# Attention in a hybrid encoder block: the softmax rows of a tile's two halves lie end to end, one transpose turns the last half block of the first with the first half block of the second, and the turned blocks lie in fixed tiles

## The chip, the cores and the metric

The kernel runs on one core of one Trainium2 chip (trn2). The metric is device time in microseconds: a program is run several times and the median is taken. Below, PE is the TensorE matmul queue, PEld its weight loads, DVE is VectorE, ACT ScalarE, POOL GpSimd, and SP the engine that issues most DMAs.

## What is computed

One encoder block over 1024 positions and 16 meta tokens, width 1024: an RMS norm, one input projection, a retention branch, an attention branch, gates, an output projection and a second norm. The change touches the attention branch alone, so that part of the reference is shown:

```python
def _windowed_sink_attention(q, k, v, sink):
    ...
    ok = (jnp.abs(qpos[:, :, None] - kp) <= WINDOW) & (kp >= CHUNK) & (kp < Lp)
    s_band = jnp.einsum("bnqgrd,bnkgd->bngrqk", qb, kb) * scale
    s_band = jnp.where(ok[None, :, None, None], s_band, NEG_INF)
    s_meta = jnp.einsum("bnqgrd,bmgd->bngrqm", qb, km) * scale
    s = jnp.concatenate([s_band, s_meta], axis=-1)
    ...
    p = jnp.exp(s - m)
    p = p / (jnp.sum(p, axis=-1, keepdims=True) + jnp.exp(sink_l - m))
    o = (jnp.einsum("bngrqk,bnkgd->bnqgrd", p[..., :3 * CHUNK], vb)
         + jnp.einsum("bngrqm,bmgd->bnqgrd", p[..., 3 * CHUNK:], vm))
```

There are 8 query heads of 128 channels, 2 key heads, 8 blocks of 128 positions, and a window of 128 positions on either side. All is float32. The kernel keeps that precision by splitting an operand into a rounded high part and the rest (names that end in h and l), so that a product takes three matmuls: high by high, low by high, high by low (`mm3`).

## The kernel before

The program runs in stages on one core: projections and retention first (up to about 335 us), then attention (about 335 to 546 us), then the gate projections, the two branch projections and the output projection. In the last stages PE multiplies 512 columns at a time.

**The attention.** A tile is a pair of heads `hp` (four of them) and a block `n` (eight), so 32 tiles. A tile has two sides `x_` of 128 rows, each of 64 queries of both heads. Side 0 sees the whole of block n-1, the whole of block n and the first 64 keys of block n+1; side 1, 64 positions on, sees the last 64 keys of block n-1, the whole of n and the whole of n+1. With 16 meta keys this makes 336 scores in a row (272 or 208 at the two ends).

`stage1(hp, n)` makes the scores of both sides on PE (`ps`), masks them on DVE and takes the row's extreme (`raw`, `nm`), takes exp on ACT with the row's sum (`p`, `den`), inverts the sum on DVE, scales the row on POOL, and copies the 16 meta columns twice into `pm2` on POOL. The last two tiles scale on ACT instead.

`stage2(hp, n)` turns the weights, so that keys lie on partitions. Each side's row lies in a field of 401 columns with 64 zeros at one end, so that each of the three blocks is 128 columns wide for both sides: 2 transposes for each block, 4 into the PSUM bank `t1` and 2 into `t2` (those of n+1), and one of the meta columns. For n = 0 and n = 7 there are two blocks, so 4 and one. ACT copies `t1` into `pah` (high part, 512 columns), the meta rows into `pm` and the third block into `pbh` (256 columns). DVE makes the low parts `pal`, `pm` and `pbl`.

`stage3(hp, n)` multiplies by the values: three matmuls of 256 columns for each block and one for the meta keys, summed in `po`, which ACT copies out.

**What sets the order.** The loop over the 32 tiles issues, for tile k: `stage1` of tile k+1, `stage2` of tile k, a counted number of pieces of other work (`fill`: the projections `paq` and `pak` of later heads and the products `pe` of the gates), and `stage3` of tile k-1. PE keeps that order through `follow`. So a tile's weights are turned one whole tile after its scores, and are used one tile later still. Other engines' instructions are put in order by the framework, which plans with a model of each instruction's length; a change of lengths can move instructions past one another there. POOL's queue holds the scaling of `p` and also the accumulating DMAs that rotate the queries and keys (`aq<-m_aq`, `akr<-m_ak`).

The lines that the prediction names are 1486 (mask), 1489 (exp), 1496 (inverse), 1505 (scaling), 1525, 1529 and 1530 (transposes), 1535, 1538 and 1545 (ACT's copies), 92 (DVE's low parts, a helper), 76 to 78 (`mm3`), 1560 and 1565.

## Time and profile before

| what | before |
|---|---|
| time, median of 3 runs | 1032.83 us (1031.2 to 1034.33) |
| span of the profiled execution, first to last instruction | 1029.8 us |
| DMA, moved in the span | 188.45 MB, mean 183 GB/s |
| attention (335 to 546 us): instructions on the turned tiles (`pt`) | PE 28.83, DVE 50.39, ACT 40.18 us busy |
| attention: instructions on the softmax rows (`p`) | PE 25.34, ACT 38.95, POOL 42.66 us busy |

The profile gives the span of the execution that it took and no time for what lies around it; the median of the runs is 3.0 us above that span. A busy time of PE is the sum of matmuls whose ends are modelled and which overlap: two neighbours can start 0.11 us apart and be listed with 0.27 us each, so what a matmul occupies is read from the distance of two starts in the timeline, and not from its length. A row of the timeline gives start, length, engine, source line, operation and tiles; "x4" merges four instructions that followed each other without a gap, and square brackets hold the idle time ahead of it and what ended it.

### The profile page before, as it was taken

What the parts mean: (1) busy time and instruction counts of PE and PEld (TensorE: products, weight loads), DVE (VectorE), ACT (ScalarE), POOL (GpSimd) and SP (SyncE); (2) the same over time, 40 slices, a digit from 0 to 9 for tenths busy, and PEclk for the clock granted to TensorE, in tenths of its full rate; (3) what the DMA queues carried; (4) which work ended last, traced back from release to release, by engine and by line L of the source; (5) the groups of instructions that cost most, each with busy time, mean ns of one, the idle gap of its engine ahead of it and who ended that gap; (6) DMA issues with size and microseconds to landing.
All of it is one profiled execution on the core that took longest, in us unless ns stands there. A gap on an engine that the chain in (4) does not pass through costs nothing. (4 is left out here: it accounts for less than half of the span.)

```text
span 1029.8 us, 17327 instructions
## 1 busy us (share of the span) xinstructions
PE 1019.0 (99%) x5875; PEld 898.0 (87%) x5875; DVE 834.5 (81%) x1805; ACT 505.0 (49%) x1138; POOL 228.3 (22%) x368
## 2 busy tenths in 40 slices
PE   9999999999999999999999999999999999999997
PEld 8999999989989888988888888888887888888886
DVE  7787858769866778777769999998889899778665
ACT  5632332523424566665677555455567456334442
POOL 3445244243342424443310000000000000111032
PEclk9999999999999999999999999999999999999999
DMA  9433123243241457675559689899874856889464
GB/s 354 172 88 88 62 46 89 82 88 101 80 94 62 103 164 203 177 196 163 172 175 329 204 286 326 303 320 317 273 259 145 261 197 200 246 213 354 123 122 81
DMA packets 98984, 188.45 MB, mean 183 GB/s; under 512 B 13040, under 2 KB 37648, under 8 KB 98336
## 3 DMA queue, kind: packets, MB, share of 16 engines
q1 hardware_dynamic: 81344, 162.89, 46.9%
q0 software_dynamic: 10176, 14.73, 9.5%
q10 hardware_dynamic: 7376, 9.73, 2.8%
q8 instruction: 46, 0.75, 0.3%
q14 instruction: 42, 0.34, 0.1%
HBM read 124.32 MB, written 57.68 MB: 177 GB/s over the span
## 5 line engine op out<-in xcount | busy, mean ns | idle before, releaser
L1348 POOL DMA_DIRECT2D mx_d<-c1a x4 | 3.6, 890 | 391.2 <-DMA a<-in_w_out_dram 369.3
L77 PE MATMUL bz<-big,llz 128*128 128x512 f32 x192 | 74.9, 390 | 0.2 <-DVE llz L92 0.2
L78 PE MATMUL bz<-big,lhz 128*128 128x512 f32 x192 | 74.4, 389 | 0.0
L76 PE MATMUL bz<-big,lhz 128*128 128x512 f32 x192 | 74.1, 389 | 0.0
L76 PE MATMUL pv<-wh,big 128*128 128x256 f32 x256 | 73.0, 285 | 0.0
L78 PE MATMUL pv<-wl,big 128*128 128x256 f32 x256 | 72.7, 284 | 0.0
L77 PE MATMUL pv<-wh,big 128*128 128x256 f32 x256 | 72.3, 282 | 0.0
L77 PE MATMUL bz<-T,llz 128*128 128x512 f32 x176 | 68.6, 390 | 0.6 <-DVE llz L92 0.6
L78 PE MATMUL bz<-T,lhz 128*128 128x512 f32 x176 | 68.5, 389 | 0.0
L76 PE MATMUL bz<-T,lhz 128*128 128x512 f32 x176 | 68.3, 390 | 0.0
L1505 POOL TENSOR_SCALAR p<-p,den 128x336 f32<-128x336 f32 (+2 forms) x60 | 33.0, 572 | 83.5 <-DVE den L1496 78.7
L76 PE MATMUL paq<-big,wh 128*128 128x512 f32 x128 | 51.5, 402 | 0.0
L1489 ACT ACTIVATE p<-raw,nm 128x337 f32<-128x337 f32 (+1 forms) x64 | 35.5, 556 | 32.1 <-DVE nm L1486 30.7
L77 PE MATMUL paq<-big,wl 128*128 128x512 f32 x128 | 50.3, 393 | 0.0
L78 PE MATMUL paq<-big,wh 128*128 128x512 f32 x128 | 50.3, 393 | 0.0
L76 PEld LDWEIGHTS pv<-wh,big 128*128 128x128 f32 x256 | 48.4, 189 | 0.2
L77 PEld LDWEIGHTS pv<-wh,big 128*128 128x128 f32 x256 | 48.4, 189 | 0.0
L78 PEld LDWEIGHTS pv<-wl,big 128*128 128x128 f32 x256 | 48.3, 189 | 0.0
L77 PEld LDWEIGHTS bz<-big,llz 128*128 128x128 f32 x192 | 36.0, 188 | 7.9 <-DVE llz L92 0.5
L78 PEld LDWEIGHTS bz<-big,lhz 128*128 128x128 f32 x192 | 36.1, 188 | 7.4
L76 PEld LDWEIGHTS bz<-big,lhz 128*128 128x128 f32 x192 | 36.1, 188 | 7.4
L558 ACT ACTIVATE op<-pa,rcol 128x256 f32<-128x256 f32 x32 | 15.2, 475 | 53.6 <-PE pa L78 52.7
(627 smaller groups left out, 3612.4 us busy)
## 6 DMA issues: line engine op xcount, KB each, us to landing
wrz<-in_w_in_dram SPq DMA_DIRECT2D x32, 512.0 KB, 5.7
wr<-in_w_in_dram SPq DMA_DIRECT2D x29, 512.0 KB, 3.7
we<-in_w_in_dram SPq DMA_DIRECT2D x16, 512.0 KB, 4.5
tg<-tg_d SPq DMA_DIRECT2D x32, 256.0 KB, 5.2
e<-e ACTq DMA_DIRECT2D x20, 256.0 KB, 2.8
e<-e SPq DMA_DIRECT2D x20, 256.0 KB, 4.4
xn<-in_x_dram SPq DMA_DIRECT2D x8, 512.0 KB, 9.4
oTr_d<-ost SPq DMA_DIRECT2D x16, 256.0 KB, 2.1
```

The lines of the kernel that those rows point to most:

```text
L76: nc.tensor.matmul(o, ah, bh, start=first, stop=False, **kw)
L77: nc.tensor.matmul(o, al, bh, start=False, stop=False, **kw)
L78: latest[:] = [nc.tensor.matmul(o, ah, bl, start=False, stop=last, **kw).ins]
L558: nc.scalar.activation(o, pa[:, 0:256], AF.Copy, scale=rcol[:, c:c + 1])
L1348: nc.gpsimd.dma_start(d, to, accum_op=ALU.add)
L1489: last["exp"] = nc.scalar.activation(pp[:, x_, w0 - o:w0 - o + 1 + wid], r[:, 0:1 + wid], AF.Exp, scale=-1.0, bias=nm_[:, x_:x_ + 1], accu ...
L1505: nc.gpsimd.tensor_scalar(v, v, den[:, x_:x_ + 1], 1.0, op0=ALU.mult, op1=ALU.mult)
```

## The change

The two sides' rows now lie end to end in one row of 674 columns (`weights`), side 0 in columns 1 to 336 and side 1 from column 337 on. The last 64 columns of side 0 (block n+1) and the first 64 of side 1 (block n-1) are neighbours, and one transpose turns both: on partitions 0 to 63 it has side 0's half of block n+1, on 64 to 127 side 1's half of block n-1. That makes 4 whole blocks, this shared one and the meta columns, so 6 transposes in place of 7 for n = 1 to 6. For n = 0 and n = 7 there are 5 as before; for n = 0 the shared one has 64 columns. The halves that nobody writes hold zeros, set once.

The turned blocks go into fixed tiles `pth` and `ptl` of 6 x 128 columns, one pair for even and one for odd n, in place of `pah`, `pal`, `pbh` and `pbl` from a pool of two. ACT copies the 4 whole blocks at once (3 for n = 0 and 7) and each half block, 64 partitions by 128 columns, on its own; DVE does the same for the low parts. In stage 3 a block's two sides are now two runs of 128 columns, which touch for block n and are 512 columns apart for n-1 and n+1. The number and the shape of stage 3's matmuls stay.

```diff
@@ -1441,15 +1441,21 @@
     late_mask = aw.tile([P, 320], F32, name="late_mask")[:, 0:272]
     nc.vector.memset(late_mask, 0.0)
     nc.vector.tensor_copy(late_mask[:, 192:256], mask[0][:, 272:336])
-    weights = [ap.tile([P, 2, 401], F32, name=f"p{i}") for i in range(2)]
-    for t in weights:
-        nc.vector.memset(t[:, 0, 337:401], 0.0)
-        nc.vector.memset(t[:, 1, 0:64], 0.0)
+    weights = [ap.tile([P, 674], F32, name=f"p{i}") for i in range(2)]
+    ap.tile([P, 48], F32, name="space_t")
+    turned = [[ap.tile([P, 6 * P], R, name=f"pt{s}{i}") for s in "hl"] for i in range(2)]
+    for i in range(2):
+        for t in turned[i]:
+            nc.vector.memset(t[64:128, 0:P].bitcast(F32), 0.0)
+            nc.vector.memset(t[0:64, 5 * P:6 * P].bitcast(F32), 0.0)
 
     def attention():
         oa = [None]
         raw = [aw.tile([P, 337], F32, tag=f"raw{x_}", bufs=1, name=f"raw{x_}") for x_ in range(2)]
         st1, st2 = {}, {}
+
+        def blocks_own(n):
+            return 0 if n == 0 else P if n % 2 else P + NM
 
         def window(n, x_):
 
@@ -1482,11 +1488,11 @@
                 r = raw[x_]
                 for c in ({0: (272, 336), 7: (208,)} if x_ else {0: (0,)}).get(n, ()):
                     nc.vector.tensor_copy(r[:, c:c + 1], nsink[:, hp:hp + 1])
-                o, w0 = (0, 64) if x_ else (1, 1)
+                o, w0 = (0, 337) if x_ else (1, 1)
                 scored = nc.vector.tensor_tensor_reduce(r[:, o:o + wid], s[:, 0:wid], seen, -SCALE,
                                                         nsink[:, hp:hp + 1], ALU.add, ALU.min, nm_[:, x_:x_ + 1]).ins
 
-                last["exp"] = nc.scalar.activation(pp[:, x_, w0 - o:w0 - o + 1 + wid], r[:, 0:1 + wid], AF.Exp,
+                last["exp"] = nc.scalar.activation(pp[:, w0 - o:w0 - o + 1 + wid], r[:, 0:1 + wid], AF.Exp,
                                                    scale=-1.0, bias=nm_[:, x_:x_ + 1],
                                                    accum_out=den[:, x_:x_ + 1]).ins
                 sides.append((wid, w0, blocks, moff))
@@ -1498,13 +1504,13 @@
             both = ap.tile([P, 2, 2, NM], F32, tag="pm2", bufs=2, name=f"pm2_{hp}_{n}")
             ends = hp == 3 and n > 5
             for x_, (wid, w0, _, _) in enumerate(sides):
-                v = pp[:, x_, w0:w0 + wid]
+                v = pp[:, w0:w0 + wid]
                 if ends:
                     softmax.append(nc.scalar.activation(v, v, AF.Copy, scale=den[:, x_:x_ + 1]).ins)
                 else:
                     nc.gpsimd.tensor_scalar(v, v, den[:, x_:x_ + 1], 1.0, op0=ALU.mult, op1=ALU.mult)
             for x_, (_, w0, _, moff) in enumerate(sides):
-                w_ = pp[:, x_, w0 + moff:w0 + moff + NM].unsqueeze(1).to_broadcast([P, 2, NM])
+                w_ = pp[:, w0 + moff:w0 + moff + NM].unsqueeze(1).to_broadcast([P, 2, NM])
                 if ends:
                     softmax.append(nc.scalar.copy(both[:, x_], w_).ins)
                 else:
@@ -1513,42 +1519,46 @@
                 with tc.issue_after(last["scaled"]):
                     while held:
                         held.pop(0)()
-            pt = [lambda o, x_=x_, w0=w0: pp[:, x_, w0 + o:w0 + o + P] for x_, (_, w0, _, _) in enumerate(sides)]
-            st1[hp, n] = (pt, [b for _, _, b, _ in sides], both.rearrange("p a b c -> p (a b c)"))
+            own, late = blocks_own(n), 337 - (64 if n else 0)
+            cuts = [1] * (n > 0) + [1 + own, late + own] + [late + 272] * (n < NB - 1 and n > 0) + [late + P] * (n == 0)
+            ends_ = (1 + P, 1 + P + 64) if n == 0 else (273, 273 + P)
+            st1[hp, n] = ([pp[:, c:c + P] for c in cuts], pp[:, ends_[0]:ends_[1]], both.rearrange("p a b c -> p (a b c)"))
 
         def stage2(hp, n):
-            pt, sides, both = st1.pop((hp, n))
-            blocks = sides[0]
+            full, ends_, both = st1.pop((hp, n))
             t1 = p1(f"pt1_{hp}_{n}")
-            for j in range(2):
-                for x_ in range(2):
-                    nc.tensor.transpose(t1[:, 256 * j + P * x_:256 * j + P * x_ + P], pt[x_](sides[x_][j][1]), ident)
+            c0 = 0 if n else P
+            for j, v in enumerate(full):
+                nc.tensor.transpose(t1[:, c0 + P * j:c0 + P * j + P], v, ident)
+            c1 = c0 + P * len(full)
             t2 = p1(f"pt2_{hp}_{n}")
-            if len(blocks) > 2:
-                for x_ in range(2):
-                    nc.tensor.transpose(t2[:, 256 + P * x_:256 + P * x_ + P], pt[x_](sides[x_][2][1]), ident)
+            nc.tensor.transpose(t2[0:64 if n == 0 else P, P:2 * P], ends_, ident)
             latest[:] = [nc.tensor.transpose(t2[0:4 * NM, 0:P], both, ident).ins]
-            ah = ap.tile([P, 512], R, tag="pah", bufs=2, name=f"pah{hp}_{n}")
-            al = ap.tile([P, 512], R, tag="pal", bufs=2, name=f"pal{hp}_{n}")
+            th, tl = turned[n % 2]
 
             m = pm[n % 2]
-            nc.scalar.copy(ah, t1)
+            nc.scalar.copy(th[:, P + c0:P + c1], t1[:, c0:c1])
             heads = [(slice(32 * e_, 32 * e_ + 32), slice(P * e_, P * e_ + P)) for e_ in range(2)]
             for r, c in heads:
                 last["hi"] = nc.scalar.copy(m[r, c], t2[r, 0:P]).ins
-            bl = []
-            for j in range(2):
-                bl.append((blocks[j][0], ah[:, 256 * j:256 * j + 256], al[:, 256 * j:256 * j + 256]))
-            if len(blocks) > 2:
-                bh_ = ap.tile([P, 256], R, tag="pbh", bufs=2, name=f"pbh{hp}_{n}")
-                bl_ = ap.tile([P, 256], R, tag="pbl", bufs=2, name=f"pbl{hp}_{n}")
-                last["hi"] = nc.scalar.copy(bh_, t2[:, 256:512]).ins
-                bl.append((blocks[2][0], bh_, bl_))
-            dve_lo(al, t1, ah)
+            edges = []
+            if n < NB - 1:
+                edges.append((slice(0, 64), slice(0, P)))
+            if n:
+                edges.append((slice(64, 128), slice(5 * P, 6 * P)))
+            for r, c in edges:
+                last["hi"] = nc.scalar.copy(th[r, c], t2[r, P:2 * P]).ins
+            dve_lo(tl[:, P + c0:P + c1], t1[:, c0:c1], th[:, P + c0:P + c1])
             for r, c in heads:
                 last["lo"] = dve_lo(m[64 + r.start:64 + r.stop, c], t2[r, 0:P], m[r, c])
-            if len(blocks) > 2:
-                last["lo"] = dve_lo(bl_, t2[:, 256:512], bh_)
+            for r, c in edges:
+                last["lo"] = dve_lo(tl[r, c], t2[r, P:2 * P], th[r, c])
+            bl = []
+            for b, c in ((n - 1, P), (n, 2 * P), (n + 1, 0)):
+                if 0 <= b < NB:
+                    step = P if b == n else 4 * P
+                    bl.append((b, *(t.rearrange("p (x q) -> p x q", q=P)[:, c // P:c // P + step // P + 1:step // P]
+                                    for t in (th, tl))))
             st2[hp, n] = (bl, m)
 
         def stage3(hp, n):
@@ -1556,7 +1566,8 @@
             bl, m = st2.pop((hp, n))
             po = p3(f"po{hp}_{n}")
             for j, (b, h_, l_) in enumerate(bl):
-                mm3(po[:, 0:256], *(t[:, P * g:P * g + P] for t in (vah[:, b], low_value(b))), h_, l_, j == 0, False)
+                mm3(po[:, 0:256].rearrange("p (x q) -> p x q", x=2),
+                    *(t[:, P * g:P * g + P] for t in (vah[:, b], low_value(b))), h_, l_, j == 0, False)
             latest[:] = [nc.tensor.matmul(po[:, 0:256], vm[:, P * g:P * g + P], m, start=False,
                                           stop=True).ins]
             if n % 2 == 0:
```

Where instructions stand in the built programs, at three places. First PE, the scores of tile (2, 4) and the transposes of tile (2, 3); `ps_4_1` are scores, `pt_2_3` the turned weights, `p` the softmax rows, `pm_2_3` the meta columns. Before:

```order
L77 MATMUL ps_4_1_6646<-kTh_6211,aql_1_6357 128x336
L78 MATMUL ps_4_1_6646<-kTl_6212,aqh_1_6356 128x336
L1525 MATMUL pt_2_3_6658<-ident,p_4895 128x128
L1529 MATMUL pt_2_3_6663<-ident,p_4895 128x128
L1525 MATMUL pt_2_3_6658<-ident,p_4895 128x128 x3
L1529 MATMUL pt_2_3_6663<-ident,p_4895 128x128
L1530 MATMUL pt_2_3_6663<-ident,pm_2_3_6570 64x128
```

And now:

```order
L77 MATMUL ps_4_1_6613<-kTh_6187,aql_1_6330 128x336
L78 MATMUL ps_4_1_6613<-kTl_6188,aqh_1_6329 128x336
L1532 MATMUL pt_2_3_6625<-ident,p_4895 128x128 x4
L1535 MATMUL pt_2_3_6630<-ident,p_4895 128x128
L1536 MATMUL pt_2_3_6630<-ident,pm_2_3_6540 64x128
```

Six transposes of 128 columns have become five; what stands ahead of and behind them is the same work. Over the whole program PE has 24 matmuls fewer.

Second DVE, the low parts of the same tile; `den` is the inverse of the row sums, `m_aq` and `aq` the rotation of a later head's queries, `we` a weight. Before:

```order
L1496 RECIPROCAL den_4_6639<-den_4_6639 128x2
L92 TENSOR_TENSOR pal_3_6668<-pt_2_3_6658,pah_3_6667 128x512
L92 TENSOR_TENSOR pm_4888<-pt_2_3_6663,pm_4888 32x128 x2
L92 TENSOR_TENSOR pbl_3_6673<-pt_2_3_6663,pbh_3_6672 128x256
L838 TENSOR_TENSOR we_1_6520<-we_0_6519,we_1_6520 128x4x128
L188 TENSOR_TENSOR m_aq_00_6691<-paq_00_6609,sr 128x512
L189 TENSOR_TENSOR aq_00_6690<-paq_00_6609,cr 128x512
```

And now:

```order
L1502 RECIPROCAL den_4_6606<-den_4_6606 128x2
L92 TENSOR_TENSOR ptl_4900<-pt_2_3_6625,pth_4899 128x512
L188 TENSOR_TENSOR m_aq_00_6655<-paq_00_6576,sr 128x512
L189 TENSOR_TENSOR aq_00_6654<-paq_00_6576,cr 128x512
L92 TENSOR_TENSOR pm_4888<-pt_2_3_6630,pm_4888 32x128 x2
L92 TENSOR_TENSOR ptl_4900<-pt_2_3_6630,pth_4899 64x128 x2
L838 TENSOR_TENSOR we_1_6490<-we_0_6489,we_1_6490 128x4x128
```

One instruction of 256 columns on 128 partitions has become two of 128 columns on 64 partitions, and at this tile the rotation stands ahead of them. ACT's copies change in the same way (`pbh`, 128x256, becomes two `pth`, 64x128), at every tile with n = 1 to 6.

Third POOL, around the scaling of tile (1, 6); `akr<-m_ak` are DMAs that POOL issues for the rotated keys. Before:

```order
L89 TENSOR_SCALAR pm_1_5_6026<-p_4895 128x32 x2
L193 DMA akr_0_6058<-m_ak_0_6059 64x272 x2
L1505 TENSOR_SCALAR p_4894<-p_4894,den_6_6109 128x336 x2
L193 DMA akr_1_6158<-m_ak_1_6159 64x256 x2
L89 TENSOR_SCALAR pm_1_6_6123<-p_4894 128x32 x2
```

And now:

```order
L89 TENSOR_SCALAR pm_1_5_6008<-p_4895 128x32
L193 DMA akr_0_6037<-m_ak_0_6038 64x272
L193 DMA akr_1_6134<-m_ak_1_6135 64x256 x2
L1511 TENSOR_SCALAR p_4894<-p_4894,den_6_6088 128x336 x2
L89 TENSOR_SCALAR pm_1_6_6102<-p_4894 128x32 x2
```

The scaling of tile (1, 6) now stands behind the two DMAs of `akr_1`, which it stood ahead of. From the end of attention on, some instructions of ACT, DVE and SP have changed places with neighbours, and on PE a few matmuls; their number and kinds are the same.

## The prediction

> **What bounds the kernel now.** I begin with the page: the shares of the engines and the granted clock.
>
> ```profile
> span 1029.8 us, 17327 instructions
> PE 1019.0 (99%) x5875; PEld 898.0 (87%) x5875; DVE 834.5 (81%) x1805; ACT 505.0 (49%) x1138; POOL 228.3 (22%) x368
> PEclk9999999999999999999999999999999999999999
> ```
>
> PE is busy for 1019.0 of 1029.8 us, and its clock is at its top in each slice but for rounding. A busy PE need not be an unbroken one, so the view by stages comes next: attention, then the two halves of what follows up to the last matmuls.
>
> ```profile
> 335.00:546.00 211.00, 210.33 (x1277) 187.17 (x1276) 162.56 (x417) 130.93 (x351) 71.23 (x151) 1.00 0.61 172
> 546.00:785.00 239.00, 239.00 (x1055) 197.82 (x1054) 220.09 (x363) 134.47 (x239) 0.00 (x0) 1.00 0.81 280
> 785.00:1023.00 238.00, 237.27 (x1057) 196.52 (x1055) 194.39 (x332) 108.86 (x203) 26.20 (x31) 1.00 0.69 201
> ```
>
> The columns are the stage, its length, then busy time of PE, PEld, DVE, ACT and POOL, the clock, and the DMA share and rate. In attention PE is busy 210.33 of 211.00 us, while DVE has 48 us free (211.00 - 162.56) and ACT 80. Behind attention PE is as full, with DVE at 92% in the first half (220.09 of 239). So the question is what a PE instruction less is worth, whether the other engines keep up, and whether the stages behind pass the gain on. The view of the chain that ended last reaches only the closing DVE work, so it decides nothing here.
>
> **What a transpose occupies.** The groups give its listed length, the timeline the distance of two starts (tile (0, 5)).
>
> ```profile
> L1525 PE MATMUL pt<-ident,p 128*128 128x128 f32 x128 | 19.8, 274 | 0.3 <-POOL p L1505 0.2
> L1529 PE MATMUL pt<-ident,p 128*128 128x128 f32 x48 | 9.7, 274 | 0.1
> ```
>
> ```profile
> 369.54 0.60 PE L1525 MATMUL pt<-ident,p 128*128 128x128 f32 x4
> 369.98 0.38 PE L1529 MATMUL pt<-ident,p 128*128 128x128 f32 x2
> 370.19 0.27 PE L1530 MATMUL pt<-ident,pm 128*64 128x128 f32 x1
> 370.22 0.48 PE L76 MATMUL pe<-big,weh 128*128 128x512 f32 x1
> 370.54 0.39 PE L77 MATMUL pe<-big,wel 128*128 128x512 f32 x1
> 370.77 0.40 PE L78 MATMUL pe<-big,weh 128*128 128x512 f32 x1
> ```
>
> Four start within 0.44 us (369.98 - 369.54) and two within 0.21, so six in 0.65: 0.108 us each. The listed 274 ns overlap. The transpose of the meta columns loads 64 columns where the others load 128; it and the matmul of 512 columns behind it take 0.35 (370.54 - 370.19), of which that matmul by itself has 0.23 (370.77 - 370.54). The 0.12 left are no less than a full one's 0.108, so a transpose of 64 columns is not cheaper.
>
> **The removed transposes.** One goes at each tile with n = 1 to 6, in four head pairs: 24. At n = 0 and 7 the count stays at five, and the narrow one at n = 0 saves nothing by the row above. 24 x 0.108 = **2.6 us** off PE, in a stage where PE hardly waits: the group's idle time ahead of 128 transposes is 0.3 us.
>
> The Trainium skill, page "TensorE: Matmul & The Clock Gate", section "Part 4: PE-mode transpose", gives about 275 ns for a transpose in a kernel's context and says that the full clock does not engage for it. The first agrees with the listed 274 ns here, and the second finds no support in the clock row; priced so, 24 would be 6.6 us, and the sum 1026.2.
>
> **What ACT and DVE get.** Where one copy of 128x256 was, two of 64x128 stand. The trace has none of 64x128; the nearest row has 128 columns on 32 partitions. From the timeline at tile (1, 3), with POOL's rows for later:
>
> ```profile
> 414.83 0.52 ACT L1538 CAST pm<-pt 32x128 fp32r<-32x128 f32 x2
> 415.36 0.37 ACT L1545 CAST pbh<-pt 128x256 fp32r<-128x256 f32 x1
> 415.60 0.67 DVE L92 TENSOR_TENSOR pal<-pt,pah 128x512 fp32r<-128x512 f32 x1
> 415.63 0.63 ACT L698 CAST aqh<-aq 128x512 fp32r<-128x512 f32 x1
> 416.14 1.69 POOL L193 DMA_DIRECT2D aq<-m_aq  x2 [7.67 <-ACT pbh L1545]
> 416.30 0.58 DVE L92 TENSOR_TENSOR pm<-pt,pm 32x128 fp32r<-32x128 f32 x2
> 416.90 0.42 DVE L92 TENSOR_TENSOR pbl<-pt,pbh 128x256 fp32r<-128x256 f32 x1
> 417.24 0.68 DVE L92 TENSOR_TENSOR aql<-aq,aqh 128x512 fp32r<-128x512 f32 x1
> 417.26 1.66 POOL L1505 TENSOR_SCALAR p<-p,den 128x336 f32<-128x336 f32 x2
> ```
>
> On ACT two of 128 columns take 0.53 us (415.36 - 414.83) and one of 256 takes 0.27 (415.63 - 415.36); on DVE 0.60 (416.90 - 416.30) and 0.34 (417.24 - 416.90). Each engine gets 0.26 us a tile, 24 x 0.26 = 6.2 us in all. At n = 0 and 7 a half block's copy is added and the large one loses 128 of 512 columns; that is at most another 0.3 us for each of 8 tiles, 2.4. Together 8.6 us on engines with 48 and 80 free. The bounds for a tile are 0 (a copy of 64 partitions as short as half of the large one) and 0.53 on DVE, if its low parts also wait for ACT's later copies of the same bank. Even 0.53 x 24 = 12.7 us leaves DVE room, so as throughput this costs **nothing**: PE's products of other heads cover it, and without that cover it would cost the 6.2 us. Four more memsets, ahead of attention, have DVE's own waits there to lie in.
>
> **Where it can be felt** is on tiles where PE gets to the transposes just as POOL has scaled. Three show it in PE's timeline: (1, 4), (2, 2) and (2, 3).
>
> ```profile
> 418.63 0.27 PE L1529 MATMUL pt<-ident,p 128*128 128x128 f32 x1
> 418.98 0.55 PE L1525 MATMUL pt<-ident,p 128*128 128x128 f32 x3
> ```
>
> ```profile
> 454.19 0.60 PE L1525 MATMUL pt<-ident,p 128*128 128x128 f32 x4
> 454.86 0.41 PE L1529 MATMUL pt<-ident,p 128*128 128x128 f32 x2
> ```
>
> ```profile
> 461.24 0.27 PE L1529 MATMUL pt<-ident,p 128*128 128x128 f32 x1
> 461.74 0.55 PE L1525 MATMUL pt<-ident,p 128*128 128x128 f32 x3 [0.23 <-POOL p L1505]
> ```
>
> Against 0.11 a transpose the steps are long by 0.24 (0.35 - 0.11), 0.23 (0.67 - 0.44) and 0.39 (0.50 - 0.11), 0.86 in all. The chain behind them is mask on DVE, exp on ACT, inverse on DVE, scaling on POOL, so 0.26 us more ahead of it can lengthen each stall by 0.26: 0 to 0.8 us for three. The new order also needs side 1's scaling at the third transpose, not the second, which gives 0.1 back. At tile (1, 6) POOL's scaling now stands behind two DMA issues:
>
> ```profile
> 426.87 1.07 POOL L1505 TENSOR_SCALAR p<-p,den 128x336 f32<-128x336 f32 x2 [2.98 <-DVE den L1496]
> 427.89 1.64 POOL L193 DMA_DIRECT2D akr<-m_ak  x2
> 430.61 0.60 PE L1525 MATMUL pt<-ident,p 128*128 128x128 f32 x4
> ```
>
> Swapped, the DMAs go from about 427.0, when DVE has the key, to 428.7; the scaling runs from 1.1 us after their start, as in the rows of 416.14 and 417.26, to 429.8, or 430.3 with the meta copies behind it. PE is there at 430.5. That still fits, with a price of 0 to 0.6. I take **0.4 us** for all four places, half of the 0.8, the 0.6 being covered.
>
> **Behind attention.** The gain survives if the next stage starts earlier too.
>
> ```profile
> 540.00 0.69 DVE L1057 TENSOR_TENSOR stz0S<-wrz,wrz 128x512 f32<-128x512 f32 x1 [3.37 <-PE pe L78]
> 541.52 0.40 PE L76 MATMUL bz<-big,lhz 128*128 128x512 f32 x1
> 542.08 0.50 PE L77 MATMUL bz<-big,llz 128*128 128x512 f32 x1 [0.16 <-DVE llz L92]
> 785.47 0.39 PE L76 MATMUL br<-big,lhr 128*128 128x512 f32 x1
> 786.44 0.50 PE L77 MATMUL bz<-T,llz 128*128 128x512 f32 x1 [0.58 <-DVE llz L92]
> ```
>
> DVE sat idle 3.37 us and began the next stage's operands when PE had done its last `pe` product, so that start moves with PE. PE then waits for `llz` at 542.08 (0.33 over its step of 0.23) and once more at 786.44 (0.74 over), and nowhere between, so DVE keeps ahead for 244 us. Stages behind pass the gain on, as far as those two waits are not set by a DMA.
>
> **Sum.** On the span: 1029.8 - 2.6 + 0.4 = 1027.6. The median of the runs is 3.0 above the span, so **1030.6 us**, 0.2% less than 1032.83. About 0.3%, or 3.1 us, is what a measurement of this kernel can tell from no change, and the three runs lie 3.1 apart.
>
> **Rivals.**
>
> *The gain turns into waits* (0.13). PE comes 0.11 us a tile earlier to rows that ACT and DVE finish 0.26 later, and 2.6 us earlier to `llz`. For it speaks DVE's 92% from 546 to 785, against it that PE waits only twice there. If it takes all: 1032.8.
>
> *Stalls go as well* (0.12). The framework has laid ACT, DVE and SP anew; without the 0.86 of the three tiles, the 0.33 and the 0.74, the gain is 2.6 + 1.9 = 4.5: 1028.3. Nothing in the profile says that they would go.
>
> *Transposes hold PE for their listed length* (0.05): 24 x 0.274 = 6.6, so 1026.2. The starts 0.108 apart speak against it.
>
> *The split operand reads slowly* (0.08), the case on the other side. Stage 3 now reads the edge blocks as two runs of 128 columns 2 KB apart: 14 blocks a head pair (one at n = 0 and 7, two between), three matmuls each, four pairs, 168 matmuls. The trace has only unbroken ones:
>
> ```profile
> 367.43 0.28 PE L76 MATMUL po<-pah,vah 128*128 128x256 f32 x1
> 367.55 0.28 PE L77 MATMUL po<-pah,val 128*128 128x256 f32 x1
> ```
>
> These step by 0.12 us. Broken ones cost from 0 more to 0.10 more, if they ran as two passes of 128 columns at a transpose's 0.108. I take 0, since count and columns are the same. From 0.0155 us each (2.6 / 168) the gain is gone, from 0.034 the kernel is slower by over 0.3%, and at 0.10 it gains 16.8: 1047.
>
> The Trainium skill, page "SBUF — State Buffer", section "Specifications (TRN2)", names lines of 16 bytes, each crossing to a new line paying a penalty. Runs of 512 bytes cross as many lines as an unbroken row, so by it the price is 0 and the sum stays; no run here shows such an operand yet.
>
> **How the numbers follow.** The forecast has 0.62; its own spread is 1029.4 to 1032, from the stall terms (0 to 1.4) and about 1 us for the median of three runs. About 0.10 of it lies below 1029.7, the bound for faster. Faster: 0.10 + 0.12 + 0.05 = 0.27. Slower: 0.08. Within 0.3%: 0.65. The range takes in the forecast, the gain that is lost (with the runs' spread) and most of the stalls that go: 1028.0 to 1033.5; left out are 0.08, 0.05 and some 0.04.
>
> **What would show it.** Right: 24 PE instructions fewer, transposes still 0.11 apart, attention shorter by about 2.2 us from its first to its last transpose, ACT and DVE busier by 6 to 9 us, no more idle time on PE behind 546. Wrong: `po` matmuls of the edge blocks stepping by more than 0.12; stalls ahead of `pt` that add up to over 2 us; waits for `llz` longer by what attention saved; or copies of 64x128 well over 0.3 us.

## The result, and the profile after

The changed kernel takes **1039.95 us** (median of 6 runs, 1037.1 to 1041.5), the kernel before 1032.42 beside it (1031.2 to 1034.33). The ratio is 1.0075, with a 95% interval of 1.0065 to 1.0085: slower by 0.75%, where 1030.6 was predicted. The profiled run of the change took 1037.1 us. One execution of e1, the first experiment below, took 3551.6 us and is left out of its median.

From the page of the change, the span and the busy times of the engines:

```profile
span 1035.3 us, 17319 instructions
PE 1020.0 (99%) x5851; PEld 895.6 (87%) x5851; DVE 843.5 (81%) x1841; ACT 510.1 (49%) x1170; POOL 229.5 (22%) x368
```

PE has 24 instructions fewer, as planned, DVE 9.0 us more and ACT 5.1 (predicted: 8.6 each). Yet the span grew by 5.5 us. The view by stages, with the columns of before (stage, length, busy PE, PEld, DVE, ACT, POOL, clock, DMA):

```profile
335.00:551.00 216.00, 210.39 (x1255) 184.69 (x1254) 170.64 (x448) 136.79 (x382) 72.05 (x152) 1.00 0.60 168
551.00:790.00 239.00, 238.97 (x1054) 197.29 (x1053) 219.74 (x363) 133.42 (x239) 0.00 (x0) 1.00 0.81 279
790.00:1028.00 238.00, 237.25 (x1057) 196.64 (x1056) 194.41 (x330) 108.93 (x203) 26.21 (x31) 1.00 0.70 202
```

In windows of the same lengths as before, the two stages behind show nearly the same busy times; attention needs a window 5 us longer, in which PE has the same 210.4 us. So PE idles in attention. The view of PE's waits there names whom it waits for (total, times, longest):

```profile
PE pt L1535 <- DVE ptl L92: 2.3, 5, 0.8
PE pe L77 <- DVE wel L92: 1.6, 3, 0.8
PE ps L78 <- DVE kTl L92: 0.7, 1, 0.7
PE pt L1532 <- POOL p L1511: 0.5, 1, 0.5
PE paq L77 <- DVE wl L92: 0.2, 1, 0.2
```

In the same view of before there is one line up to 542 us:

```profile
PE pt L1525 <- POOL p L1505: 0.2, 1, 0.2
```

Four of the five name DVE's low parts, 4.8 us together. The listed waits are a part only, since the matmul ahead is drawn out over some of the idle time. By the starts (what a step of two matmuls is long over that of its neighbours, counted above 0.095 us) PE stalls for some 9 us in attention, against less than 2 before. The difference of about 7.1, less the 2.6 us of 24 transposes, is the 4.5 by which attention grew.

**Where in attention.** The timeline of one tile's turn (the copies that ACT and DVE make of its turned weights, and what they wait for in each other) shows it, first DVE before, while it makes the low parts of tile (3, 1), with one row of ACT:

```profile
504.17 0.17 DVE L1496 RECIPROCAL den<-den 128x2 f32<-128x2 f32 x1 [0.87 <-ACT p L1489]
504.64 0.69 DVE L92 TENSOR_TENSOR pal<-pt,pah 128x512 fp32r<-128x512 f32 x1 [0.30 <-ACT pah L1535]
...
505.04 0.37 ACT L1545 CAST pbh<-pt 128x256 fp32r<-128x256 f32 x1
...
505.44 0.58 DVE L92 TENSOR_TENSOR pm<-pt,pm 32x128 fp32r<-32x128 f32 x2
506.04 0.43 DVE L92 TENSOR_TENSOR pbl<-pt,pbh 128x256 fp32r<-128x256 f32 x1
506.38 0.68 DVE L838 TENSOR_TENSOR we<-we,we 128x512 f32<-128x512 f32 x1
```

And after, at the same tile, with the rows of ACT and PE that matter:

```profile
507.33 0.17 DVE L1502 RECIPROCAL den<-den 128x2 f32<-128x2 f32 x1 [1.07 <-ACT p L1495]
...
507.80 0.69 DVE L92 TENSOR_TENSOR ptl<-pt,pth 128x512 fp32r<-128x512 f32 x1 [0.30 <-ACT pth L1540]
...
508.20 0.53 ACT L1550 CAST pth<-pt 64x128 fp32r<-64x128 f32 x2
...
508.76 0.58 DVE L92 TENSOR_TENSOR pm<-pt,pm 32x128 fp32r<-32x128 f32 x2 [0.27 <-ACT pth L1550]
509.36 0.59 DVE L92 TENSOR_TENSOR ptl<-pt,pth 64x128 fp32r<-64x128 f32 x2
...
509.98 0.69 DVE L838 TENSOR_TENSOR we<-we,we 128x512 f32<-128x512 f32 x1
...
510.10 0.30 PE L1535 MATMUL pt<-ident,p 128*128 128x128 f32 x1 [0.83 <-DVE ptl L92]
```

DVE's queue runs in order and waits for ACT twice in each turn: 0.87 us for exp, 0.30 for the high part. From the first low part to the next operation it takes 1.74 us before (506.38 - 504.64) and 2.18 after (509.98 - 507.80): **0.44 us a tile more**. Of these, 0.26 are the second short operation, as predicted, and most of the rest is a wait that has grown. In both kernels `pm` starts 0.03 us after ACT's last copy out of the same PSUM bank (505.04 + 0.37 before, 508.20 + 0.53 now). That is now the second half-block copy, and the gap ahead of `pm` is 0.27 where it was 0.11. The bank of the shared transpose is free only when the last `ptl` is done, so PE stands 0.83 us ahead of line 1535.

Why did DVE's 48 us free not take this up? The groups of before (DVE, from 335 to 542 us; the numbers behind the bar are busy time, mean ns, idle time ahead and what ended it) tell:

```profile
L92 DVE TENSOR_TENSOR pal<-pt,pah 128x512 fp32r<-128x512 f32 x31 | 21.3, 687 | 6.8 <-ACT pah L1535 6.8
L92 DVE TENSOR_TENSOR pm<-pt,pm 32x128 fp32r<-32x128 f32 x62 | 17.7, 285 | 3.1 <-ACT pbh L1545 0.3
...
L1496 DVE RECIPROCAL den<-den 128x2 f32<-128x2 f32 x30 | 4.9, 164 | 17.8 <-ACT p L1489 17.8
```

17.8 + 6.8 + 3.1 = 27.7 us of it are waits inside that turn. They recur with each tile whatever DVE still has to do, so they were not room.

### The profile page after: what moved, and what is told of

The parts are those of the page before. It is cut to its first block, busy times and chain, and to the rows that moved or that the text cites. A ratio compares the mean times of both kernels' runs of the same rounds, so it can differ in the third digit from the quotient of the medians.

```text
span 1035.3 us, 17319 instructions
## 1 busy us (share of the span) xinstructions
PE 1020.0 (99%) x5851; PEld 895.6 (87%) x5851; DVE 843.5 (81%) x1841; ACT 510.1 (49%) x1170; POOL 229.5 (22%) x368
## 5 line engine op out<-in xcount | busy, mean ns | idle before, releaser
L92 DVE TENSOR_TENSOR ptl<-pt,pth 64x128 fp32r<-64x128 f32 (+2 forms) x88 | 37.1, 422 | 6.8 <-ACT pth L1540 6.0
```

The costliest lines, as they stand in the source:

```text
L92: return nc.vector.tensor_tensor(o, i, hi.bitcast(F32), ALU.subtract).ins
```

## The experiments

Below, *attention* runs from the first meta transpose of tile (0, 0) to the first `bz` product, *behind* from there to the last matmul; both, and the times of the head pairs, are read in one profiled execution of each kernel. The two profiles of the change differ by 0.7 us in attention and by 2.9 behind, so a difference behind is used only where the medians bear it out; the profile of e10 is of a run 2.5 us under its median. The times are medians against the kernel before in the same batch, whose median was 1031.9 to 1032.5. *Head pair 3* runs from the last transposes of tile (3, 0) to those of (3, 7).

| run | us | ratio, 95% interval | attention | of it up to (3, 0) | head pair 3 | behind |
|---|---|---|---|---|---|---|
| before | 1032.42 | | 205.88 | 160.01 | 44.93 | 481.04 |
| after | 1039.95 | 1.0075 [1.0065, 1.0085] | 210.36 | 160.95 | 48.83 | 481.80 |
| e1 short copies alone | 1035.64 | 1.0032 [1.0020, 1.0045] | 209.87 | 161.82 | 47.11 | 480.10 |
| e2 after, one copy | 1033.16 | 1.0013 [1.0004, 1.0021] | 204.92 | 157.95 | 45.94 | 485.22 |
| e3 fewer transposes alone | 1033.53 | 1.0013 [1.0004, 1.0021] | 205.86 | 158.60 | 46.34 | 482.32 |
| e4 after, sums on POOL | 1040.20 | 1.0070 [1.0057, 1.0084] | 208.86 | 163.36 | 44.91 | 484.18 |
| e5 after, no sums | 1033.70 | 1.0014 [1.0005, 1.0022] | 205.34 | 159.84 | 44.92 | 483.26 |
| e6 before, no sums | 1031.09 | 0.9990 [0.9981, 0.9998] | 205.73 | | | 480.28 |
| e7 after, sums in the wait | 1034.23 | 1.0020 [1.0011, 1.0028] | 206.00 | 160.51 | 44.91 | 482.99 |
| e8 before, sums in the wait | 1031.17 | 0.9987 [0.9978, 0.9995] | 205.18 | 159.75 | 44.51 | 480.73 |
| e9 after, own block first | 1039.36 | 1.0069 [1.0057, 1.0081] | 210.69 | | | 483.92 |
| e10 e7 and own block first | 1034.39 | 1.0024 [1.0015, 1.0034] | 206.28 | | | 481.11 |
| e11 e3, sums in the wait | 1031.52 | 0.9995 [0.9986, 1.0004] | 203.29 | 158.29 | 44.08 | 484.26 |
| e12 after once more | 1038.24 | 1.0064 [1.0050, 1.0077] | 209.67 | 160.40 | 48.69 | 484.74 |
| e13 e11 and 24 idle transposes | 1031.75 | 0.9995 [0.9986, 1.0003] | 206.82 | 161.82 | 44.08 | 480.26 |
| e14 e8 and 24 | 1034.39 | 1.0020 [1.0011, 1.0029] | 208.10 | | | 481.42 |
| e15 e3 and 24 | 1031.90 | 0.9999 [0.9990, 1.0008] | 205.80 | 160.74 | 44.13 | 481.05 |
| e16 after and 24 | 1037.87 | 1.0056 [1.0043, 1.0068] | 209.33 | | | 483.66 |
| e17 e7 and 24 | 1035.71 | 1.0032 [1.0021, 1.0043] | 208.72 | | | 482.82 |

The theories, as the expectations name them: the **ring** or turn of DVE and ACT just described; the **order** into which the framework lays the other engines; DVE's **throughput**; **transfers** that set the pace whatever the engines do; the **split operand**, which is the prediction's rival of two runs that read slowly; later, a **late order** of the stages behind that the changed last tile brings, and a pace that **PE** sets.

**e1: the short copies alone.** The kernel before, with its two transposes of the third block, and two copies of 64x128 into zeroed fixed tiles. The other halves are not copied. For side 0 that half holds zeros; for side 1 it is the first 64 keys of block n+1, which this kernel leaves out.

```diff
-                last["hi"] = nc.scalar.copy(bh_, t2[:, 256:512]).ins
+                for r, c in edges:
+                    last["hi"] = nc.scalar.copy(bh_[r, c], t2[r, 256 + c.start:256 + c.stop]).ins
...
-                last["lo"] = dve_lo(bl_, t2[:, 256:512], bh_)
+                for r, c in edges:
+                    last["lo"] = dve_lo(bl_[r, c], t2[r, 256 + c.start:256 + c.stop], bh_[r, c])
```

> The kernel before, all transposes kept; only the copy of the third block (128x256) is made as two copies of 64x128 on ACT and two on DVE, into fixed tiles cleared once (half of one block and half of the other are not copied). Ring theory (in late attention DVE and ACT wait for each other once a tile, in an order that is fixed, so what is added to their copies lengthens the tile and PE waits): nothing is taken off PE, so slower than before by the 5.5 us that the changed kernel lost plus the 2.6 us it saved, 7 to 8 us: 1039 to 1041. Order theory (the loss is from m_aq, aq and xs work that the framework moved ahead of the copies): about half of that, 1034 to 1037. Split-operand theory: no broken operand here, 1032.4.

**e2: the change with one copy.** At n = 1 to 6 a single copy of 128x128; side 1's half of block n-1 then stays zero, so that part of the sum is left out (it lands in side 0's half of block n+1).

```diff
-            if n:
+            if n == NB - 1:
                 edges.append((slice(64, 128), slice(5 * P, 6 * P)))
+            elif n:
+                edges = [(slice(0, 128), slice(0, P))]
```

> The changed kernel, but for n = 1 to 6 the shared block is copied once, 128x128, into one block of the fixed tile in place of two copies of 64x128 into two (block 5 stays zero, so its half block is left out of the sum). PE has the same instructions as the changed kernel, the operand in two runs too. Ring theory: ACT and DVE get one copy no longer than the 128x256 of before, the stalls go back to those of before and the 2.6 us come out: 1029 to 1031. Order theory: the DVE order around m_aq of tile (2,3) is nearly that of the changed kernel, so 1038 to 1040. Split-operand theory: 1040.

**e3: the removed transposes alone.** The kernel before; at n = 1 to 6 only side 0's third block is turned, and the copies read it twice, in their old shape. Side 1's third block thus holds side 0's.

```diff
-                for x_ in range(2):
+                for x_ in range(2 if n == 0 else 1):
                     nc.tensor.transpose(t2[:, 256 + P * x_:256 + P * x_ + P], pt[x_](sides[x_][2][1]), ident)
...
+                    third = t2[:, 256:384].unsqueeze(1).to_broadcast([P, 2, P])
```

> The kernel before with 24 transposes fewer and nothing else: at n = 1 to 6 only side 0's third block is turned, and the copies read it twice (side 1's third block is left out). All copies keep their size. Ring theory: 2.6 us fewer on PE as far as DVE and ACT keep up, 1029.8 to 1031.5. If late attention is already as long as the ring, PE gains less there and the time stays at 1031.5 to 1032.4. Order theory: the framework moves a few DVE instructions here as well, so some of the loss shows: 1033 to 1036.

The copies alone lengthen attention by 4.0 us (209.87 - 205.88), and put on top of the fewer transposes by 4.5 (210.36 - 205.86). The transposes alone bring attention nothing (205.86 against 205.88), though PE reaches (3, 0) 1.4 us earlier: head pair 3 takes the gain back (46.34 against 44.93). In e2, where PE stalls hardly longer than before up to there, it is 2.06 earlier, 18 x 0.114, so the transposes do free what was predicted. By the times alone e1 and e3 fit the order (1034 to 1037, 1033 to 1036), not the ring (1039 to 1041, 1029.8 to 1031.5). But e2 has the rotation `m_aq` ahead of the low parts at (2, 3), as the changed kernel has, and its operand in two runs, and takes 1033.16: the order's 1038 to 1040 and the split operand's 1040 fall. A smaller share of the order stays possible, since e2's sums `xs` stand as they did before. In e2 attention gains 1.0 (204.92 against 205.88) and the time is still 1.3 above that of its batch (1031.9), not the ring's 1029 to 1031: the stages behind give 4.2 back in its profile, which was 2.1 above its median. So the copies are the main cost, and something behind attention adds to it.

e2's one copy has as many columns as each half block's, on twice the partitions, yet its steps are shorter (tile (3, 1)):

```profile
504.91 0.27 ACT L1552 CAST pth<-pt 128x128 fp32r<-128x128 f32 x1
505.07 0.59 ACT L869 COPY e<-pe 128x512 f32<-128x512 f32 x1
```

ACT goes on after 0.16 us, and DVE after 0.21. From the first low part to the end of the last, e2's turn takes 1.61 us at most tiles, where it was 1.83 before and is 2.15 with the change.

**e4: the sums on POOL.** DVE also adds the gates' weights in attention (`we`, line 838), 12 sums in the late part. They go to POOL.

```diff
-                nc.vector.tensor_tensor(v, a, b, op)
+                (nc.gpsimd if 8 < u < 13 else nc.vector).tensor_tensor(v, a, b, op)
```

> The changed kernel, but the 12 sums we (128x512) of four weight parts between tiles (2,3) and (3,4) run on POOL, which is idle there, not on DVE: 12 x 0.61 = 7.3 us of DVE work out of the ring, nothing else left out. Ring theory: the stalls of late attention shrink by most of their 8 us, 1031 to 1035, unless POOL comes late with its scaling, which stands behind these sums. Order theory: m_aq stays ahead of the copies in part, 1036 to 1039. Split-operand theory: 1040.

**e5 and e6: the sums left out,** in the changed kernel and in the one before.

```diff
-        pre_sums(u, (i,))
+        if not 8 < u < 13:
+            pre_sums(u, (i,))
```

> The changed kernel without the 12 sums we (128x512) of four weight parts between tiles (2,3) and (3,4): they are left out, so 12 x 0.61 = 7.3 us of DVE work go and POOL gets nothing. PE, POOL and the copies keep their order. Ring theory (DVE and ACT take turns within a tile, and with these sums the turn is as long as PE's work on the tile): the stalls from tile (2,3) to (3,6), 6.4 us in the profile of the changed kernel, fall under 2: 1034 to 1036. Transfer theory (late attention is paced by the weight transfers that the casts wait for): the transfers stay, so 1038 to 1040.

> The kernel before without the same 12 sums. Ring theory: PE waits there for under 1 us in all, so little is to be had: 1030.5 to 1031.9, and the distance between the two kernels without sums is 3 to 4 us where it is 8 with them. Transfer theory: 1031.9, and a distance of 8.

**e7 and e8: the same sums inside DVE's wait for exp.** Nothing is left out. They are issued behind the masks, where DVE waits 0.87 us a tile.

```diff
     def pre_sum(u, i):
-        pre_sums(u, (i,))
+        gaps.append(lambda: pre_sums(u, (i,))) if 8 < u < 13 else pre_sums(u, (i,))
...
+                if gaps:
+                    gaps.pop(0)()
             last["sum"] = nc.vector.reciprocal(den, den).ins
```

> The changed kernel with the same 12 sums kept on DVE, but each issued behind the masks of a tile and ahead of the inverse, where DVE waits some 0.87 us for ACT's exp; what of them is left when the parts are cast goes there as before. Nothing is left out. Ring theory: a sum of 0.61 fits into that wait, so that about 9 of the 12 cost the turn nothing: the stalls of late attention shrink by half or more, 1034 to 1037. Throughput theory (DVE simply has more work than time, wherever it stands): the same work, so 1039 to 1040.

> The kernel before with the 12 sums in DVE's wait for exp, in the same way. Nothing is left out. Ring theory: what PE waits in late attention (0.4 at (2,3), 0.3 for wel) goes: 1031 to 1031.9, at most 0.1% less. Throughput theory: 1031.9.

e5 comes near the ring's 1034 to 1036 and far from 1038 to 1040, and e7 not near the throughput theory's 1039 to 1040. 12 sums of 0.69 us are 8.3 us of DVE. If DVE's throughput were the limit, moving them could not help. They stay in e7, and head pair 3 is as short as without them (44.91 and 44.92, against 48.83). The timeline of e8 shows one in the wait:

```profile
502.22 0.56 DVE L1490 CUSTOM_DVE_ANT_0 raw<-ps,mask,nsink 128x336 f32<-128x336 f32 x1
...
502.76 0.69 DVE L838 TENSOR_TENSOR we<-we,we 128x512 f32<-128x512 f32 x1
504.12 0.17 DVE L1502 RECIPROCAL den<-den 128x2 f32<-128x2 f32 x1 [0.67 <-ACT p L1493]
```

DVE's idle time ahead of the inverse falls in e8's groups from 17.8 to 14.5 us:

```profile
L1502 DVE RECIPROCAL den<-den 128x2 f32<-128x2 f32 x30 | 4.9, 163 | 14.5 <-ACT p L1493 14.4
```

e5 and e6, without the sums, are 2.6 us apart, under the ring's 3 to 4 and far from the transfers' 8. So waits in the turn can be used, but only by work that is put into them. In the kernel before, where the turn was not yet the limit, the sums are worth 1.2 us in all (e8 and e6). **e8 is the version that beats both,** by 0.13% over before, with its interval below 1. On POOL (e4) they gain nothing (1040.20, above both the ring's 1031 to 1035 and the order's 1036 to 1039; the ring's condition, that POOL not come late, did not hold): head pair 3 is relieved as much (44.91), but 3.4 us are lost before it against before's 160.01, and PE now waits for POOL:

```profile
PE pt L1536 <- POOL pm L89: 2.3, 2, 1.2
PE pt L1532 <- POOL p L1511: 1.6, 2, 1.0
```

A sum of 1.29 us there stands between two short meta copies that PE waits for:

```profile
513.80 0.21 POOL L89 TENSOR_SCALAR pm<-p 128x32 f32<-128x32 f32 x1
514.06 1.29 POOL L838 TENSOR_TENSOR we<-we,we 128x512 f32<-128x512 f32 x1
515.33 0.22 POOL L89 TENSOR_SCALAR pm<-p 128x32 f32<-128x32 f32 x1
```

e7 takes back 5.7 of the 7.5 us; 1.8 over before stay, with attention no longer than before. The next runs look for these.

**e9 and e10: the order of the last tile's blocks.** The change sums block n-1 first. For the last tile its own block is put first, without and with e7's sums.

```diff
+            if (hp, n) == (3, NB - 1):
+                bl.sort(key=lambda t: t[0] != n)
```

> The changed kernel, and in stage 3 of tile (3,7) alone the tile's own block is multiplied ahead of its neighbour's, nothing else: the first product there then does not wait for the late copy of the edge block, and the framework lays the stages behind attention nearly as it did before (6 lines of difference on SP where the changed kernel has 70, 11 on DVE for 147). Attention keeps its order. Theory of the late order (the order of the stages behind, not attention, costs the kernels built from the changed one 1 to 3 us more from the first product behind attention to the last): 1037 to 1038.5. Ring theory alone: 1039.5 to 1040.5.

> The changed kernel with both edits: the 12 sums in DVE's wait for exp, and the own block first in stage 3 of (3,7). Nothing is left out. Ring theory with the theory of the late order: 1034.2 less 2 to 3, 1031 to 1032.5. Ring theory alone: 1034.2.

Nothing changes (1039.36 and 1034.39), so the late order theory fell. **e11** is e3 with e8's sums, and **e12** the changed kernel once more.

> The kernel before with 24 transposes fewer (side 1's third block left out at n = 1 to 6, its copies kept at full size) and the 12 sums in DVE's wait for exp. Ring theory: with the ring shortened PE is the bound again, so the transposes are worth their 2.6 us here: the sums alone gave 1031.2, so 1028.5 to 1030. If 24 transposes are worth nothing for another reason: 1031.2. In the trace the first product behind attention stands 1.5 to 2.6 us earlier, counted from the first tile's last transpose, than with the sums alone.

> The changed kernel once more, for a second profile: the first one came from a run of 1037.1, the fastest of six with a median of 1039.95. Ring theory with the theory of the late order: attention as long as in the first profile (210.4 us from the first tile's last transpose to the first product behind), and if the run takes 1039 or more, the 2 to 3 us are behind attention, in waits for weights that land late (481.8 us in the first profile, 484 to 485 in this one). Ring theory alone: the 2 to 3 us are in attention.

In e11 the gain of the transposes at last arrives at the end of attention: 203.29 against e8's 205.18, 1.9 us of the 2.6. But the time is 1031.52, not the 1028.5 to 1030 expected nor below e8's 1031.17: behind, its profile (0.75 above its median) takes 3.5 us longer (484.26 against 480.73). In e12 the profiled run takes 1039.12, 2.0 more than that of the first profile; attention is 0.7 us shorter, so the difference lies behind (484.74), as the late order's account had it, though e9's remedy did nothing.

**e13 to e17: 24 idle transposes given back at one place,** tile (2, 7), written to a part of the bank that nobody reads. PE has before's number of instructions again, and what the copies and the order cost is kept.

```diff
+            if (hp, n) == (2, NB - 1):
+                for _ in range(24):
+                    nc.tensor.transpose(t2[:, 256:256 + P], pt[0](sides[0][0][1]), ident)
```

> The kernel of e11 (24 transposes fewer, sums in the gap) with 24 transposes of a block already turned put back at tile (2,7), into a part of the bank that nobody reads: PE has as many as before, 2.6 us of them in one place ahead of head pair 3. Theory that the stages behind are paced by their transfers: the first product behind attention moves from 203.3 to 205.2 to 205.9 us after the first tile's last transpose, the stages behind shrink from 484.3 to about 481.5, and the time stays at 1031 to 1031.8. Theory that PE paces the stages behind and something else lengthens them: 1033.5 to 1034.1.

> The kernel of e8 (the kernel before with the sums in the gap) with the same 24 idle transposes at (2,7). There the first product behind attention stood at 205.2 us. Pacing by transfers: the transfers have slack for less than 1 us there, so of the 2.6 us 1.5 to 2.6 show, 1032.7 to 1033.8. PE pacing: 1033.8.

> The kernel of e3 (24 transposes fewer, sums where they were) with the same 24 idle transposes at (2,7). Ring theory: in e3 PE had lost its 1.4 us of lead by waits in head pair 3; the idle work takes that lead away ahead of head pair 3, and PE is then 1.2 us late there, so attention ends 0 to 1.2 us later than in e3; with transfers pacing the stages behind the time is 1033 to 1034. PE pacing throughout: 1036.

> The changed kernel with 24 idle transposes of a block already turned put back at tile (2,7): 2.6 us of PE work in one place, the saving undone, everything else kept. Ring theory: PE waits 4 to 5 us in head pair 3 for DVE and ACT, so idle work ahead of it lies in those waits: 1037 to 1040, no more than the 1038.2 to 1040 of the changed kernel. If PE's count paces the time, it rises by 2.6: 1041 to 1042.5.

> The changed kernel with the sums in the gap (e7) and the same 24 idle transposes at (2,7). Its attention was ring-bound only at a few tiles, so some of the 2.6 us show in attention (0.5 to 2.6), but the stages behind, 483.0 us in e7, shrink towards 480 to 481 if they are paced by transfers: 1033 to 1035. PE pacing: 1036.8.

e13 shows what the saving is worth: the idle transposes cost attention 3.5 us, more than the 2.6 counted, so the stages behind start that much later than in e11, and they end at the same time (1031.75 us, within the 1031 to 1031.8 of the transfers). First e11's start, PE's chief waits behind and the load of a weight unit ahead of them, in its timeline:

```profile
539.01 0.40 PE L76 MATMUL bz<-big,lhz 128*128 128x512 f32 x1
...
743.51 1.62 SPq L1283 DMA_DIRECT2D wrz<-in_w_in_dram  x3
...
751.44 0.62 ACT L1023 CAST lhz<-wrz 128x512 fp32r<-128x512 f32 x1 [4.07 <-PE bz L78]
...
752.11 0.50 PE L76 MATMUL bz<-big,lhz 128*128 128x512 f32 x1 [0.67 <-ACT lhz L1023]
...
752.84 0.49 PE L77 MATMUL bz<-big,llz 128*128 128x512 f32 x1 [0.22 <-DVE llz L92]
```

Then the same in e13:

```profile
542.57 0.40 PE L76 MATMUL bz<-big,lhz 128*128 128x512 f32 x1
...
744.28 1.67 SPq L1283 DMA_DIRECT2D wrz<-in_w_in_dram  x3
...
750.99 0.62 ACT L1023 CAST lhz<-wrz 128x512 fp32r<-128x512 f32 x1 [2.79 <-DMA wrz<-in_w_in_dram]
```

e11 starts 3.56 us earlier, but the load goes out only 0.77 earlier and takes longer to land. The views of the tile `wrz` (735 to 755 us) give the time from issue to landing, smallest, median and largest, first of e11, then of e13:

```profile
DMA to landing us min/median/max: 7.8/8.5/9.1
```

```profile
DMA to landing us min/median/max: 6.6/7.2/7.9
```

The cast comes even 0.45 later, and PE waits where it does not wait in e13. The row of e11's cast names PE as what ended the wait, but the load landed at 751.3 (743.51 + 7.8), 0.10 ahead of the cast, as in e13 (744.28 + 6.6). By the starts PE stalls 4.4 us behind attention in e11 and 0.55 in e13; that is nearly the difference of the stages (484.26 - 480.26 = 4.0). The DMA engines are busy 0.81 of their time there.

The same load decides in every profile, and did so in the kernel before:

```profile
750.75 0.62 ACT L1019 CAST lhz<-wrz 128x512 fp32r<-128x512 f32 x1 [2.81 <-DMA wrz<-in_w_in_dram]
751.40 0.69 DVE L92 TENSOR_TENSOR llz<-wrz,lhz 128x512 fp32r<-128x512 f32 x1 [2.80 <-ACT lhz L1019]
```

In all 19 profiles its cast begins 0.10 us after it has landed. From the low part that follows (751.40 here), DVE works 56.8 us without a gap, and the last matmul starts 271.2 to 271.3 us after it (271.6 in e6 and e10). So what PE saves ahead of it counts only as far as this load comes earlier. It is issued when a transfer of `z` has landed, 201.6 to 206.1 us after the first `bz` product, and lands 5.9 to 7.8 us later.

The other four show the same from their side. 2.6 us of PE work cost 3.2 in e14 over e8, 1.5 in e17 over e7, nothing in e16 over the change, and e15 is 1.6 *below* e3, where no theory had less than 1033. In e14 the deciding load goes out 2.4 us later than in e8 (746.75 against 744.33) and lands 3.5 later. e14, e15 and e17 missed their ranges for the transfers theory by 0.6, 1.1 and 0.7, and all four missed those for PE's pace, so neither theory alone accounts for them; e16 lies in the ring's 1037 to 1040.

## Why the prediction was wrong

**Right.** A transpose frees about 0.11 us: PE was 2.06 us earlier after 18 of them (e2). The Trainium skill, page "TensorE: Matmul & The Clock Gate", section "Part 4: PE-mode transpose", gives about 275 ns; the listed 274 ns agrees with it, but as what a transpose occupies it would have made 4.95 us, and the trace disagrees. The short operations take 0.27 us on ACT and 0.30 on DVE, and the second one adds 0.26 a tile, as worked out. The swap at (1, 6) cost nothing. And the operand in two runs costs nothing. The last of them in a tile of the change, three products of the edge block and that of the meta keys:

```profile
506.97 0.28 PE L76 MATMUL po<-pth,vah 128*128 128x256 f32 x1
507.09 0.28 PE L77 MATMUL po<-pth,val 128*128 128x256 f32 x1
507.21 0.28 PE L78 MATMUL po<-ptl,vah 128*128 128x256 f32 x1
507.32 0.28 PE L1571 MATMUL po<-pm,vm 128*128 128x256 f32 x1
```

They step by 0.11 to 0.12 us, as the unbroken ones did. By the Trainium skill, page "SBUF — State Buffer", section "Specifications (TRN2)", with its penalty for each crossing to a new line, the price was worked out as 0, and the trace agrees. The rival on the slower side therefore fell, and the kernel is slower for another reason.

**Near by luck.** POOL's stalls at the three tiles grew by 0.17 us, inside the 0 to 0.8 that was given, but not as worked out. At (1, 4) they are 0.85 where 0.24 stood, more than the 0.26 allowed for one tile; at (2, 3) they are 0.18 where 0.39 stood; and the 0.23 at (2, 2) is gone. At (2, 3) PE also loses 0.64 us to DVE, for which the sum had no term. DVE has 1.34 us of the sums `xs` ahead of the low parts there, where it had 0.41 before, so this one wait goes back to the framework's new order:

```profile
462.18 0.30 PE L1535 MATMUL pt<-ident,p 128*128 128x128 f32 x1 [0.48 <-DVE ptl L92]
```

**The step that failed** is "Together 8.6 us on engines with 48 and 80 free", and "as throughput this costs nothing". The size was inside its bounds: 0.44 us a tile, where 0 to 0.53 stood, the upper end for just this wait on ACT's later copies. What was wrong is the cover. DVE's free time was counted over the stage, while 27.7 of the 48 us were waits of the tile's own turn with ACT. In head pair 3 PE has 6.4 us of work for a tile (44.93 / 7), and 0.44 us more in the turn reached PE, so the turn had less slack than that over it; with the sums out of the turn (e5, e7) head pair 3 is as long as before again, though some 0.75 us of stalls stay in it. The copies cost attention 4.0 to 4.5 us, more than half of it there (e1: 2.2 of 4.0). The change grows there by 3.9, where 7 x 0.44 is 3.1; the rest was not traced to single rows. The passage "Where it can be felt" went by tiles where PE waits for POOL before, and not by those where DVE's turn had no slack left. The prediction's own sign of being wrong, stalls ahead of `pt` of over 2 us, came: 2.3 and 0.5 us are listed.

**The second failed step** is "Stages behind pass the gain on". The condition stood beside it, as far as the waits for `llz` "are not set by a DMA", and it did not hold. DVE has no gap between the low part at 751.40, which waited for a load, and the `llz` of 786 in the trace of before, so the later of the two waits is set by a DMA there already. "DVE keeps ahead for 244 us" was read from PE's waits alone.

**The nearest rival** was "The gain turns into waits": the place was right, ACT and DVE late and PE waiting. But its price was capped at the gain (1032.8), as if a wait could only eat what was saved. Its own price, 24 x 0.44 = 10.6 us less what is still hidden, goes past it.

**What stays open.** The stages behind take 0.8 and 3.7 us longer in the two profiles of the change, and 1.3 in e3, against before's 481.04. In e15 PE has its work back and they are as long as before (481.05), so it goes with the earlier or uneven PE. It comes in through the load named above; why that load's issue, counted from the first `bz` product, differs by 4.5 us between the kernels was not found. Own-block-first did not change it.

## What to carry to other kernels

An engine's free time in a stage is room only outside the waits that recur in a fixed turn with another engine; price an edit by the length of that turn against the bound engine's work for one tile. Saved time of the bound engine counts up to the next stage that is paced by its loads, so ask there whether the loads can start earlier too. Where a turn contains a wait, put other work into it, as e8 does.

## What the runs showed of the hardware

In a pair, a copy of 64x128 is hardly cheaper than one of four times the elements: steps of 0.27 us on ACT and 0.30 on DVE, against 0.27 and 0.34 for 128x256. So the two halves cost nearly double. It is not the size alone, as the single half blocks of the change show, first at (2, 0) on partitions 0 to 63, then at (2, 7) on 64 to 127:

```profile
445.99 0.26 ACT L1550 CAST pth<-pt 64x128 fp32r<-64x128 f32 x1
446.15 1.05 ACT L118 CAST wh<-wr 128x1024 fp32r<-128x1024 f32 x1
...
495.37 0.26 ACT L1550 CAST pth<-pt 64x128 fp32r<-64x128 f32 x1
495.65 1.05 ACT L848 CAST weh<-we 128x1024 fp32r<-128x1024 f32 x1
```

Behind the first, ACT goes on after 0.16 us, as behind e2's 128x128; behind the second only when the copy's 0.26 us are over. In a pair the upper half likewise begins only when the lower one has ended. So here a copy overlapped with the next instruction where both began at partition 0, and not where one of the two began at 64; no run tests whether that is the reason.

Idle work may also make a kernel faster: with 24 transposes that nobody reads, e3 went from 1033.53 to 1031.90. The runs come from two batches, and the intervals against before (1.0004 to 1.0021 and 0.9990 to 1.0008) overlap a little.
